# Moving one of layer 0's background modulation groups in gate/up to layer 1's projections and gate/up, in a one-core encoder trunk

## The chip, the cores and the metric

The kernel runs on one core of one Trainium2 chip. The metric is the device time of one execution in microseconds, the median of several runs. A profile of one execution, taken by the hardware profiler, stands beside it.

## The reference

Two layers of a bidirectional encoder over 1024 tokens of width 1024, in fp32. Each layer draws six vectors of length 1024 (the modulation: shift, scale and gate for the attention part and for the feed-forward part) from a condition vector `c`. A group, in this document, is one such vector of one layer: group `(l, g)` is layer `l`'s vector number `g` from 0 to 5.

```
cond = silu(c)                                   # (1024,)
for l in range(2):
    mod = cond @ w_mod[l] + b_mod[l]             # (6 * 1024,): a matrix of 1024 x 6144
    sh_a, sc_a, gt_a, sh_f, sc_f, gt_f = split(mod, 6)     # groups (l, 0) .. (l, 5)
    h = rms_norm(x, g_attn[l]) * (1 + sc_a) + sh_a
    proj = h @ w_in[l]
    y = concat of three attention groups (neighbourhood, sliding window, dense), each normalized
    x = x + gt_a * (y @ w_o[l])
    h = rms_norm(x, g_ffn[l]) * (1 + sc_f) + sh_f
    gate, up = split(h @ w_gu[l], 2)             # two times 2816 columns
    x = x + gt_f * ((silu(gate) * up) @ w_down[l])
return rms_norm(x, g_final)
```

## The kernel before

**Matmuls.** Every fp32 operand is split into a high part, rounded for the fast matmul, and a low part, the rest; a product is three matmuls (high x high, low x high, high x low). ScalarE (ACT) makes the high parts by a copy, VectorE (DVE) or GpSimd (POOL) the low parts by a subtraction. The helper that records every operation is line 49, so the profile puts all of them on L49; they are told apart by their tiles.

**Gate/up.** The product of `h` with `w_gu` is cut by a Strassen-like scheme into seven products for each of 22 blocks of columns, counted by `q` (even `q` a gate block, odd `q` the up block that belongs to it). The seven are listed in `PRODUCTS` (line 218) and run in the order h11, h21, ht2, ht1, ht3, h22, ht4, named for the operand made from `h`; their place in the list is `i`, 0 to 6. One product of one `q` is called a unit here: 12 matmuls into a PSUM tile `ps_w` (`product`, `gu_product`). ACT reads the results out of PSUM (tile `u`, or `sg`) and takes the Silu; DVE and POOL add the pieces, multiply gate by up (tiles `u` and `sg`), and the finished blocks are stored to DRAM (`gpd`) through SyncE's queue (SP). The weights of a block arrive in `wr` through the same queue; DVE makes the sums of weight blocks (`ws`), and ACT, DVE and POOL their high and low parts (`wpt`), a few units ahead (`Ahead.fill`). A product waits for its `wpt` parts, and for ACT to have read the PSUM tile that it writes into.

The first seven blocks (`EARLY = 7`) have their first two products done ahead of the loop; from `q = 7` on a block's seven units follow each other, 105 units in all.

**Modulation beside it.** Groups are worked off in the order of a list `todo`. The first two of layer 0 are computed at the start. The others run in the background, as a matrix-vector product on DVE: a load of a piece of `w_mod` (tile `wmt`), then `acc += wmt * cond[k]` on DVE, and when a group's rows are through, a sum over the 128 partitions. That sum (`mod_parts`, line 325, and `mod_flush`, line 334) is: DVE copies half of `acc` to `acch` and subtracts to get `accl`; PE multiplies both with a matrix of ones (tile `ps_mod`, two matmuls, one reduction pair); DVE multiplies by the identity and reduces along the free axis (`sums`); then the same for the other half. `mod_finish` adds the bias, and for a scale group (g = 1 or 4) one product gives `gsc`.

There are two places for this work. In a layer's projections (`mod_one`, line 1082) 24 steps of one row block each work off three groups per layer. In gate/up `mod_stream` (line 358) is a generator that is advanced one step at a time behind a unit:

```
            halves = [(k, c0) for k in range(first, KC) for c0 in range(0, 1024, width)]
            ...
            for i, (k, c0) in enumerate(halves):
                if i + 1 < len(halves):
                    load(i + 1)
                mod_add(k, acc[:, c0 : c0 + width], loads.pop(i))
                yield
            going["step"] = KC
            mod_parts(slice(0, width), shared)
            while going["step"]:
                yield
                yield
                mod_flush(psp)
            yield
```

`width` is 512, so a group has 16 halves. A group takes 22 steps: one that only loads, 16 adds, and five for the two reduction pairs. `mod_parts` issues the copies `acch` and `accl`; two steps later `mod_flush` issues the pair on PE that reads them, and in the same step `mod_parts` for the second half. The loads go into a tag with two buffers, so the load of a half waits for the add two before it.

**What sets the order.** Instructions are issued in program order, one queue per engine, and in gate/up a scheduling layer may reorder ACT's, DVE's, POOL's and PE's; SP's order is pinned to the program's in this loop (`pin([sp], True)`), so every load and store of gate/up, of `wr`, `gpd` and `wmt`, stands in one line. An engine's instructions start in the order of its queue. In the loop a unit's product comes first, then `ahead.fill()`, then `g_step()` (a piece of the block's finishing), then the modulation step (line 2060).

The loop before, line 2015 and lines 2059 to 2062: the stream runs up to, not including, group (1, 3), in whichever layer; a step follows every unit from `q = 7` on; what is left is run off behind the loop.

Of the kernel before, what the change touches and what calls it, by code (L numbers as in the profile page):

```python
# [23 lines left out]
H = 512  # L24
# [61 lines left out]
def trunk(ctx: ExitStack, tc, A, C, out):  # L86
# [9 lines left out]
    def open_pool(name, bufs=1, side="left", space=None):  # L96
        kw = dict(name=name, bufs=bufs, side=side, reuse_waits="tile")
        if space is not None:
            kw["space"] = space
            if space == PSUM:  # L100
                kw.pop("side")
        cm = tc.tile_pool(**kw)
        p = cm.__enter__()
        return cm, p
# [200 lines left out]
    def mod_add(k, acc, st):  # L305
        ck = condT[:, k : k + 1]
        if k == 0:
            dve.tensor_scalar(out=acc, in0=st, scalar1=ck, scalar2=None, op0=ALU.mult)
        else:
            dve.scalar_tensor_tensor(  # L310
                out=acc, in0=st, scalar=ck, in1=acc, op0=ALU.mult, op1=ALU.add
            )
# [12 lines left out]
    def mod_parts(c, shared):  # L325
        pl, tag, bufs, width = shared
        acc = going["acc"]
        hi = pl.tile([P, width], F32R, name="acch", tag=tag, bufs=bufs)
        lo = pl.tile([P, width], F32R, name="accl", tag=tag, bufs=bufs)
        dve.tensor_copy(hi, acc[:, c])  # L330
        dve.tensor_tensor(out=lo, in0=acc[:, c], in1=f32(hi), op=ALU.subtract)
        going["parts"] = c.start, hi, lo, shared

    def mod_flush(psp):

        if going["step"] < KC:
            return
        acc, (c0, hi, lo, shared) = going["acc"], going["parts"]
        width = shared[3]
        if c0 == 0:  # L340
            going["sums"] = cp.tile([P, 8], F32, name="sums", tag="sums")
        sums = going["sums"]
        for o in range(0, width, H):
            ps = psp.tile([P, 4, P], F32, name="ps_mod", tag="mm")
            row = ps.rearrange("p a b -> p (a b)")
            pe.matmul(row, onesr, hi[:, o : o + H], start=True, stop=False)
            pe.matmul(row, onesr, lo[:, o : o + H], start=False, stop=True)
            d = acc[:, c0 + o : c0 + o + H].rearrange("p (a b) -> p a b", a=4)
            dve.tensor_tensor(out=d, in0=ps, in1=bc(ident[:, None, :], [P, 4, P]), op=ALU.mult)
            n = (c0 + o) // P  # L350
            dve.tensor_reduce(out=sums[:, n : n + 4], in_=d, axis=AX.X, op=ALU.add)
        if c0 + width < 1024:
            mod_parts(slice(c0 + width, c0 + 2 * width), shared)
            return
        mod_finish(*todo.pop(0), sums)
        going["step"] = 0

    def mod_stream(psp, shared, until):


        pl, tag, bufs, width = shared
        acc = None
        while todo and todo[0] < until:
            l, g = todo[0]
            first = going["step"]
            if first == 0:
                going["acc"] = cp.tile([P, 1024], F32, name="acc", tag="acc")
            acc = going["acc"]
            halves = [(k, c0) for k in range(first, KC) for c0 in range(0, 1024, width)]
            loads = {}  # L370

            def load(i):
                k, c0 = halves[i]
                st = loads[i] = pl.tile([P, width], F32, name="wmt", tag=tag, bufs=bufs)
                g0 = g * 1024 + c0
                sp.dma_start(st, A["w_mod"][l, k * P : (k + 1) * P, g0 : g0 + width])

            if halves:
                load(0)
# [13 lines that stand above are left out]
# [140 lines left out]
    ps_cm, psl = open_pool("ps0", bufs=8, space=PSUM)  # L533
# [285 lines left out]
    for l in range(2):  # L819
# [353 lines left out]
        for oc in range(NE, 8):  # L1173
            w = wab
            for half in range(2):
# [3 lines left out]
                if oc == 6 and half == 0:  # L1179
                    close(ps_cm)  # L1180
                    psS_cm, psS = open_pool("psS", bufs=2, space=PSUM)
                    ps_cm, psl = open_pool("ps2", bufs=4, space=PSUM)
# [8 lines left out]
                i = 2 * (oc - NE) + half  # L1191
# [404 lines left out]
        for n in range(-AHEAD - 1, N + 3):  # L1596
# [70 lines left out]
            for end, (chunks, width) in norms.items():  # L1667
                if begins[end] <= m <= end and (m - begins[end]) % 8 == 7 and (n <= NC or m >= NC):
                    i = (m - begins[end]) // 8
# [29 lines left out]
        ps_cm, psl = open_pool("ps1", bufs=4, space=PSUM)  # L1699
# [65 lines left out]
        nt_cm, ntp = open_pool("nt", side="left")  # L1765
# [80 lines left out]
        ps_cm, psl = open_pool("ps3", bufs=8, space=PSUM)  # L1846
# [110 lines left out]
        def g_step():  # L1957
            if steps:
                steps[0].pop(0)()
                if not steps[0]:  # L1960
                    steps.pop(0)
# [6 lines left out]
        def gu_start(b):  # L1968
            g_finish(1)
            sg[b] = [x_tile(4 + 2 * (b % 2) + i, [P, S], "sg") for i in range(2)]  # L1970
# [11 lines left out]
        EARLY = 7  # L1982
# [29 lines left out]
            shifted_sub(b21, b21, shift(2 * i + 1), t2)  # L2012
            h_split("t4", i, b21, dve)

        mods_due = mod_stream(psl, (ntp, "sq", 2, H), (1, 3))
        bs = []
        rows = None
        norm = rstd_rows(ssq, ntp, psl)
# [24 lines left out]
        for q in range(NF):  # L2043
            if q % 2 == 0:
                gu_start(q // 2)
            if q < EARLY:
                up = q % 2
                e = sg[q // 2][0][:, 0:H]
                if up:
                    (pool if q > 1 else dve).tensor_tensor(  # L2050
                        out=e, in0=e, in1=quads[q]["11"], op=ALU.mult
                    )
            for i, p in enumerate(PRODUCTS[2 if q < EARLY else 0 :]):
                gu_product(q, p, ahead.get())
                if i == 1 and q < EARLY and not up:
                    act.activation(e, quads[q]["11"], AF.Silu)
                ahead.fill()
                g_step()
                if q >= EARLY:
                    next(mods_due, None)  # L2060
        for _ in mods_due:
            pass
# [30 lines left out]
        nt_cm, ntp = open_pool("nt", side="left")  # L2093
# [134 lines left out]
        for u in range(NU):  # L2228
            i, t = divmod(u, NB)
# [161 lines left out]
```

## Time and profile before

| | |
|---|---|
| median of 3 runs | 2412.68 us (2412.14 to 2415.06) |
| profiled execution | 2419.0 us, span 2417.2 us |
| mean granted TensorE clock | 0.991 |
| busy share of the span: PE, DVE, ACT, POOL | 97%, 73%, 49%, 31% |
| gate/up from the first to the last ps_w matmul, layer 0 | 586.6 to 1023 us |
| the same, layer 1 | 1763.5 to 2187 us |

In a timeline row stand the start in us, the length, the engine, the operation with output and input tiles, and in brackets the idle time ahead of it with what ended it. Matmuls are pipelined: one is shown with about 0.39 us, while the next starts 0.23 us later, so the distance between starts is what counts. A row of the waits has the engine and tile, what it waited for, the us in total, the number of times and the longest.

### The profile page before, as it was taken

What the parts mean: (1) busy time and instruction counts of PE and PEld (TensorE: products, weight loads), DVE (VectorE), ACT (ScalarE), POOL (GpSimd) and SP (SyncE); (2) the same over time, 40 slices, a digit from 0 to 9 for tenths busy, and PEclk for the clock granted to TensorE, in tenths of its full rate; (3) what the DMA queues carried; (4) which work ended last, traced back from release to release, by engine and by line L of the source; (5) the groups of instructions that cost most, each with busy time, mean ns of one, the idle gap of its engine ahead of it and who ended that gap; (6) DMA issues with size and microseconds to landing.
All of it is one profiled execution on the core that took longest, in us unless ns stands there. A gap on an engine that the chain in (4) does not pass through costs nothing.

```text
span 2417.2 us, 33362 instructions
## 1 busy us (share of the span) xinstructions
PE 2343.7 (97%) x11733; PEld 1957.8 (81%) x11733; DVE 1756.8 (73%) x2788; ACT 1194.7 (49%) x2250; POOL 744.0 (31%) x719
## 2 busy tenths in 40 slices
PE   8999999999999999999999999999999999999998
PEld 4777899888788787788787879988888888888886
DVE  5756898977967788587578579988797545447865
ACT  3421688954543333344444138897454333334443
POOL 1430345720144444300037114465004444430001
PEclk9999999999999999999999999999999999999999
DMA  8478215254245454596433861151534332329633
GB/s 264 143 235 274 71 27 133 58 178 149 92 144 179 157 182 153 158 285 191 138 110 97 282 198 32 27 161 61 196 99 160 116 101 96 121 90 298 212 129 109
DMA packets 305336, 356.95 MB, mean 148 GB/s; under 512 B 51964, under 2 KB 221788, under 8 KB 305168
## 3 DMA queue, kind: packets, MB, share of 16 engines
q1 hardware_dynamic: 283296, 342.07, 44.5%
q10 hardware_dynamic: 21504, 12.59, 2.0%
q8 instruction: 92, 1.51, 0.2%
q14 instruction: 76, 0.62, 0.1%
q0 software_dynamic: 368, 0.17, 0.0%
HBM read 269.79 MB, written 88.63 MB: 148 GB/s over the span
## 4 chain that ended last, share of the span: by engine, by line
PE 45%; DVE 5%; issue 4%; DMA 4%; ACT 3%; POOL 1%; SPq 0%; ACTq 0%; POOLq 0%; DVEq 0%
PE ps_w L49 21%; PE ps_d L49 11%; PE ps_o L49 3%; PE pv L49 2%; PE T L49 2%; PE ps_v L49 2%; PE sC L49 2%; DMA qkd<-qko 1%; DVE wpt L49 1%; ACT pr L49 1%; DMA w<-in_w_down_dram 1%; PE ps_c L49 1%; DMA cst<-const_rope_dram 1%; DMA graw<-gpd 1%; DVE xb L49 0%
## 5 line engine op out<-in xcount | busy, mean ns | idle before, releaser
L49 PE MATMUL ps_d<-wpt 128*128 128x512 f32 x1848 | 424.3, 390 | 4.0 <-ACT wpt L49 3.4
L49 PEld LDWEIGHTS ps_d<-wpt 128*128 128x128 f32 x1848 | 345.5, 188 | 78.1 <-issue 3.3
L49 POOL TENSOR_SCALAR pr<-pr,rs 128x1024 f32<-128x1024 f32 (+2 forms) x248 | 193.7, 794 | 219.3 <-DVE rs L49 190.3
L49 POOL TENSOR_TENSOR sg<-sg,u 128x512 f32<-128x512 f32 x82 | 116.5, 1421 | 353.6 <-ACT sg L49 227.8
L49 PE MATMUL pv<-pt,vs 128*128 128x256 f32 x1088 | 175.5, 296 | 17.2 <-DVE y L49 13.3
L49 DVE TENSOR_TENSOR pt<-T,pt 128x512 fp32r<-128x512 f32 x272 | 176.8, 678 | 7.4 <-ACT pt L49 7.1
L49 ACT CAST wpt<-w 128x512 fp32r<-128x512 f32 x154 | 95.9, 622 | 170.5 <-PE ps_d L49 153.1
L49 ACT CAST pt<-T 128x512 fp32r<-128x512 f32 x272 | 152.3, 585 | 40.7 <-PE T L49 38.6
L49 ACT COPY u<-ps_w 128x512 f32<-128x512 f32 x128 | 75.2, 587 | 189.9 <-PE ps_w L49 189.9
L49 POOL TENSOR_TENSOR wpt<-ws,wpt 128x512 fp32r<-128x512 f32 x80 | 110.4, 1381 | 186.2 <-ACT wpt L49 139.8
L49 DVE TENSOR_TENSOR wpt<-w,wpt 128x512 fp32r<-128x512 f32 x154 | 109.4, 710 | 79.5 <-ACT wpt L49 79.3
L49 PEld LDWEIGHTS pv<-pt,vs 128*128 128x128 f32 x1088 | 141.4, 189 | 30.0 <-DVE y L49 25.6
L49 PE MATMUL T<-identr,pr 128*128 128x128 f32 x1176 | 161.6, 273 | 0.9 <-DVE edge L49 0.4
L49 DVE SCALAR_TENSOR_TENSOR acc<-wmt,condT,acc 128x512 f32<-128x512 f32 (+1 forms) x98 | 117.2, 1204 | 47.0 <-DMA wmt<-in_w_mod_dram 46.3
L49 PEld LDWEIGHTS T<-identr,pr 128*128 128x128 f32 x1176 | 137.9, 140 | 16.1 <-issue 1.4
L49 ACT CAST wpt<-ws 128x512 fp32r<-128x512 f32 x176 | 108.1, 624 | 59.8 <-issue 28.2
L49 DVE TENSOR_TENSOR wpt<-ws,wpt 128x512 fp32r<-128x512 f32 x96 | 81.8, 861 | 62.1 <-ACT wpt L49 62.0
L49 DVE TENSOR_TENSOR wpt<-graw,wpt 128x512 fp32r<-128x512 f32 x154 | 110.3, 716 | 21.3 <-ACT wpt L49 21.1
L49 ACT CAST wpt<-graw 128x512 fp32r<-128x512 f32 x154 | 95.2, 618 | 60.0 <-DMA graw<-gpd 50.5
L49 DVE TENSOR_REDUCE rs<-sC 128x1 f32<-128x1024 f32 x88 | 107.3, 1221 | 17.8 <-PE sC L49 13.7
L49 DVE TENSOR_TENSOR ws<-wr 128x512 f32<-128x512 f32 x88 | 78.9, 899 | 54.2 <-POOL wpt L49 51.1
L49 PE MATMUL sC<-qk 128*128 128x512 f32 x384 | 108.9, 407 | 6.4 <-ACT pr L49 6.4
(300 smaller groups left out, 5945.7 us busy)
## 6 DMA issues: line engine op xcount, KB each, us to landing
wr<-in_w_gu_dram SPq DMA_DIRECT2D x92, 512.0 KB, 4.2
gpd<-sg SPq DMA_DIRECT2D x154, 256.0 KB, 4.4
graw<-gpd SPq DMA_DIRECT2D x76, 512.0 KB, 3.5
w<-in_w_down_dram SPq DMA_DIRECT2D x110, 256.0 KB, 5.1
wmt<-in_w_mod_dram SPq DMA_DIRECT2D x48, 512.0 KB, 6.1
qk<-qkd SPq DMA_DIRECT2D x44, 512.0 KB, 6.6
wst<-in_w_o_dram SPq DMA_DIRECT2D x32, 512.0 KB, 3.9
wmt<-in_w_mod_dram SPq DMA_DIRECT2D x64, 256.0 KB, 3.7
```

What stands on the lines that cost most here:

```text
L49: ins = op(*args, **kwargs)
```

## The change

```
-        mods_due = mod_stream(psl, (ntp, "sq", 2, H), (1, 3))
+        mods_due = mod_stream(psl, (ntp, "sq", 2, H), (1 + l, 2 - 2 * l))
...
                 ahead.fill()
                 g_step()
-                if q >= EARLY:
+                if q >= EARLY and i % 3 != 2:
                     next(mods_due, None)
         for _ in mods_due:
             pass
```

The bound of the stream is (1, 2) in layer 0 and (2, 0), the end of the list, in layer 1. Layer 0's projections do three groups as before, (0, 2) to (0, 4). Its gate/up did four, (0, 5) and (1, 0) to (1, 2); now it does three, up to (1, 1). Layer 1's projections did (1, 3) to (1, 5); now they do (1, 2) to (1, 4). Layer 1's gate/up, which did none, does (1, 5), the gate of the last residual. In gate/up no step follows the units i = 2 and i = 5, so five of a block's seven units have one.

The first place is DVE's queue in layer 0's gate/up, in the two reductions of the first group there, (0, 5): `acch` and `accl` are the copies that PE's pair reads, `acc<-ps_mod` is the reading of a pair's result, `ws` and `wpt` are weights, `sg` and `u` are gate/up's results. Before, from the first half's low part on:

```order
854 L49 TENSOR_TENSOR accl<-acc,acch 128x512
855 L49 TENSOR_TENSOR wpt<-ws,wpt 128x512
856 L49 TENSOR_TENSOR ws<-wr 128x512
857 L49 TENSOR_TENSOR ws<-ws,wr 128x512
858 L49 TENSOR_TENSOR wpt<-ws,wpt 128x512
859 L49 TENSOR_TENSOR ws<-wr 128x512
860 L49 TENSOR_TENSOR ws<-wr,ws 128x512
861 L49 TENSOR_TENSOR u<-u,ps_w 128x512
862 L49 TENSOR_TENSOR acc<-ps_mod,identr 128x512
863 L49 COPY acch<-acc 128x512
864 L49 TENSOR_REDUCE sums<-acc 128x4
865 L49 TENSOR_TENSOR accl<-acc,acch 128x512
```

And now, from the last rows ahead of the second half's copy to the reading of its pair:

```order
870 L49 TENSOR_TENSOR ws<-wr,ws 128x512
871 L49 TENSOR_TENSOR sg<-sg,ps_w 128x512
872 L49 TENSOR_TENSOR wpt<-wr,wpt 128x512
873 L49 COPY acch<-acc 128x512
874 L49 TENSOR_TENSOR acc<-ps_mod,identr 128x512
875 L49 TENSOR_TENSOR accl<-acc,acch 128x512
876 L49 TENSOR_REDUCE sums<-acc 128x4
877 L49 TENSOR_TENSOR wpt<-wr,wpt 128x512
878 L49 TENSOR_TENSOR u<-u,ps_w 128x512
879 L49 TENSOR_TENSOR acc<-ps_mod,identr 128x512
```

The second half's copy stood behind the first pair's reading; it now stands ahead of it, and the low part ahead of the reduction. Between the first half's `accl` (row 862 now) and the second half's `acch` stand ten rows where there were eight, over three units where there were two.

The second place is SP's queue in layer 1's gate/up, from `q = 7` on. Before:

```order
403 L49 DMA gpd<-sg 128x512 x7
404 L49 DMA wr<-in_w_gu_dram 128x4x256 x2
405 L49 DMA gpd<-sg 128x512
406 L49 DMA wr<-in_w_gu_dram 128x4x256 x2
407 L49 DMA gpd<-sg 128x512 x6
408 L49 DMA wr<-in_w_gu_dram 128x4x256 x2
```

Now:

```order
401 L49 DMA gpd<-sg 128x512 x7
402 L49 DMA wr<-in_w_gu_dram 128x4x256 x2
403 L49 DMA wmt<-in_w_mod_dram 128x512 x3
404 L49 DMA gpd<-sg 128x512
405 L49 DMA wmt<-in_w_mod_dram 128x512
406 L49 DMA wr<-in_w_gu_dram 128x4x256 x2
407 L49 DMA gpd<-sg 128x512 x2
408 L49 DMA wmt<-in_w_mod_dram 128x512
409 L49 DMA gpd<-sg 128x512
410 L49 DMA wmt<-in_w_mod_dram 128x512 x2
411 L49 DMA gpd<-sg 128x512 x3
412 L49 DMA wmt<-in_w_mod_dram 128x512 x2
```

The loads of the moved group stand between the stores of gate/up's results and the loads of its weights, which the queue had to itself in this layer.

More of the change, by code (lines that the diff above doesn't have):

```diff
@@ L2013, in t4_part @@
             h_split("t4", i, b21, dve)
-        mods_due = mod_stream(psl, (ntp, "sq", 2, H), (1, 3))
+        mods_due = mod_stream(psl, (ntp, "sq", 2, H), (1 + l, 2 - 2 * l))
         bs = []
@@ L2058, in trunk @@
                 g_step()
-                if q >= EARLY:
+                if q >= EARLY and i % 3 != 2:
                     next(mods_due, None)
```

## The prediction

> **What bounds the kernel now.** I read the page first, then the chain that ended last, then the busy time by stretches, then the PE timeline of both layers.
>
> ```profile
> PE 2343.7 (97%) x11733; PEld 1957.8 (81%) x11733; DVE 1756.8 (73%) x2788; ACT 1194.7 (49%) x2250; POOL 744.0 (31%) x719
> PE 45%; DVE 5%; issue 4%; DMA 4%; ACT 3%; POOL 1%; SPq 0%; ACTq 0%; POOLq 0%; DVEq 0%
> ```
>
> PE is busy for 97% of the span, so a change that leaves PE's work alone can only gain where PE stands still or runs at less than its pace. The change touches gate/up from the eighth unit column (q = 7) on, in both layers. The windows compare these stretches: 724 to 1016 is layer 0 with four modulation groups beside it, 1900 to 2177 is layer 1 with none. The columns are us, PE, PEld, DVE, ACT and POOL busy, granted clock, DMA share, GB/s. The third row is the same view for the instructions on the tile wmt (the modulation adds) alone.
>
> ```profile
> 724.00:1016.00 292.00, 286.70 (x1251) 235.32 (x1251) 218.19 (x268) 105.48 (x188) 123.71 (x85) 0.99 0.49 160
> 1900.00:2177.00 277.00, 277.00 (x1224) 229.37 (x1223) 134.62 (x168) 106.42 (x187) 114.41 (x85) 1.00 0.32 104
> 724.00:1016.00 292.00, 65.48 (x64) 0.99 0.49 160
> ```
>
> DVE works 218.2 of 292 us in layer 0 and 134.6 of 277 us in layer 1; PE has no idle time at all in layer 1's stretch. The PE timeline gives the exact length: first matmul of q = 7, and the ht3 product of the last q, which are 102 products apart in both layers.
>
> ```profile
> 724.05 0.62 PE L49 MATMUL ps_w<-h11h,wpt 128*128 128x512 f32 x2
> ...
> 1013.86 0.61 PE L49 MATMUL ps_w<-ht3h,wpt 128*128 128x512 f32 x2
> ...
> 1900.35 0.61 PE L49 MATMUL ps_w<-h11h,wpt 128*128 128x512 f32 x2
> ...
> 2177.79 0.62 PE L49 MATMUL ps_w<-ht3h,wpt 128*128 128x512 f32 x2
> ```
>
> Layer 1 takes 277.44 us, 2.72 us a unit; layer 0 takes 289.81 us for the same products. The four groups thus cost PE 12.37 us, and this is all that the change can play with. Where they lie:
>
> ```profile
> 778.46 0.39 PE L49 MATMUL ps_mod<-acch,onesr 128*128 128x512 f32 x1
> 778.69 0.39 PE L49 MATMUL ps_mod<-accl,onesr 128*128 128x512 f32 x1
> 778.92 0.63 PE L49 MATMUL ps_w<-ht4h,wpt 128*128 128x512 f32 x2
> ...
> 784.17 0.39 PE L49 MATMUL ps_w<-h11l,wpt 128*128 128x512 f32 x1
> 785.73 0.51 PE L49 MATMUL ps_mod<-acch,onesr 128*128 128x512 f32 x1 [1.18 <-DVE acch L49]
> 787.70 0.54 PE L49 MATMUL ps_mod<-accl,onesr 128*128 128x512 f32 x1 [1.46 <-DVE accl L49]
> 788.04 1.05 PE L49 MATMUL ps_w<-h21h,wpt 128*128 128x512 f32 x2
> ...
> 792.38 0.62 PE L49 MATMUL ps_w<-ht2h,wpt 128*128 128x512 f32 x2
> ...
> 910.63 0.39 PE L49 MATMUL ps_w<-ht2l,wpt 128*128 128x512 f32 x1
> 911.51 0.50 PE L49 MATMUL ps_mod<-acch,onesr 128*128 128x512 f32 x1 [0.49 <-DVE acch L49]
> 912.71 0.50 PE L49 MATMUL ps_mod<-accl,onesr 128*128 128x512 f32 x1 [0.69 <-DVE accl L49]
> 913.04 0.63 PE L49 MATMUL ps_w<-ht1h,wpt 128*128 128x512 f32 x2
> ...
> 967.84 0.40 PE L49 MATMUL ps_mod<-accl,onesr 128*128 128x512 f32 x1
> 969.71 0.73 PE L49 MATMUL ps_w<-ht2h,wpt 128*128 128x512 f32 x2 [1.47 <-ACT u L49]
> ```
>
> Without a wait matmuls start 0.23 us apart, and a reduction pair takes 778.46 to 778.92, 0.46 us; eight pairs are 3.68 us. The pair at 785.73 comes late: 1.33 us before it (784.17 to 785.73 less 0.23), 1.74 inside it, 0.11 behind it, and the next product takes 788.04 to 792.38, 4.34 us in place of 2.72, another 1.62. That is 4.80 us. The pair at 911.51 loses 0.65 + 0.97 + 0.10 = 1.72. At 969.71 a product waits 1.87 less 0.23 = 1.64 for ACT. Together 8.16 us; 12.37 - 3.68 - 8.16 = 0.53 stays unassigned.
>
> The 1.62 us come from the granted clock, in the columns of the windows above:
>
> ```profile
> 784.00:788.00 4.00, 1.36 (x5) 0.62 (x4) 4.00 (x6) 1.10 (x2) 2.53 (x2) 1.00 0.08 27
> 788.00:792.00 4.00, 4.00 (x12) 3.09 (x11) 2.79 (x6) 0.00 (x0) 0.00 (x0) 0.57 0.79 271
> ```
>
> PE worked 1.36 of 4.00 us, and the four us behind were granted 0.57 of the clock.
>
> Why DVE is late: it is in order, and an add that waits for its load holds the copies acch and accl that PE then waits for. ACT's late reading is the same lag at second hand; a Silu there waited for DVE and four other operations stood behind it, one of them the reading that PE needed.
>
> ```profile
> DVE acc L49 <- DMA wmt<-in_w_mod_dram: 42.2, 27, 5.2
> ...
> 967.54 0.64 ACT L49 ACTIVATE sg<-sg 128x512 f32<-128x512 f32 x1 [6.91 <-DVE sg L49]
> ...
> 969.07 0.59 ACT L49 COPY u<-ps_w 128x512 f32<-128x512 f32 x1
> ```
>
> DVE in layer 0's stretch is therefore taken for 218.2 + 42.2 = 260.4 of 292 us, 89%.
>
> **The change part by part.** *The group that leaves layer 0.* On DVE a group is 16 adds and the two reductions. The adds of four are 65.5 us, the reductions of four are these rows:
>
> ```profile
> L49 DVE TENSOR_TENSOR accl<-acc,acch 128x512 fp32r<-128x512 f32 x8 | 7.8, 974 | 0.0
> L49 DVE TENSOR_REDUCE sums<-acc 128x4 f32<-128x512 f32 x8 | 5.4, 680 | 0.1
> L49 DVE TENSOR_TENSOR acc<-ps_mod,identr 128x512 f32<-128x512 f32 x8 | 5.4, 680 | 0.0
> L49 DVE CAST acch<-acc 128x512 fp32r<-128x512 f32 x8 | 5.0, 625 | 0.0
> ```
>
> So (65.5 + 7.8 + 5.4 + 5.4 + 5.0) / 4 = 22.3 us a group, and a quarter of the waits, 10.5 us. Layer 0 goes from 260 of 292 us to about 228 of 284 (80%), layer 1 from 135 of 277 to 134.6 + 22.3 + 10.5 = 167 of 280 (60%). On PE the two pairs go from one layer to the other: -0.92 and +0.92, net nothing, whatever the cover.
>
> *The step in five of seven units.* A group is 22 steps, of which the last five hold both reductions; from the copies to the pair that reads them are two steps. Before, two steps were always two units, 5.4 us. Now they are three units (8.2 us) or two, by where the left-out units i = 2 and i = 5 fall: 3 and 2 in layer 0's first group, 2 and 3 in the second, 3 and 3 in the third, 3 and 2 in layer 1. Three groups need 66 steps of 75, so they end at unit 92 of 105 rather than at 88, still ahead of the down projection; layer 1's group ends by its unit 30 (30 x 2.72 = 82 us after 1900), and its result, the gate of the last residual, is read behind 2186. So lateness costs nothing there.
>
> *The waits.* The lag that PE met at 785.73 and 911.51 was 3.07 and 1.62 us (waits before and inside the pair). Two things work against it: a unit more (2.72 us) in five of the eight pairs, and DVE at 80% and 60% in place of 89%. In the pairs that keep two units I count on the second alone: over 5.4 us nine hundredths of DVE are 0.5 us, but the backlog that stands when the copies come is built over a whole group, 16 adds that now come every 3.8 us in place of 2.72. Per term: the 4.80 is between 0 (the first group's second pair still has two units) and 4.80, and I take 4.80, since the first pair now has three units and hands on no lag; the 1.72 likewise goes (three units in the third group). The 1.64 behind ACT I leave: it hangs on a Silu behind one DVE sum, not on the two steps; one in four groups has it. For the moved group in layer 1 I bound such a wait by 0 (layer 1's row without groups) and 1.64, and take 0.9, near the middle, for it is a whole group with its loads but on an emptier DVE.
>
> *SP.* The moved group brings 16 loads of 256 KB to layer 1's queue, between the loads of the next weights (wr) and the stores of gate/up; each add's buffer holds up what is queued behind its load. In layer 0 this queue carried 64 of them:
>
> ```profile
> SPq L49 <- DVE acc L49: 43.4, 39, 3.2
> wmt<-in_w_mod_dram SPq DMA_DIRECT2D x64, 256.0 KB, 3.7
> ```
>
> 43.4 us of such holding in 39 cases, and yet no PE wait above names a load of weights. Layer 1 gets a quarter of that, and I cost it at nothing; the cover is that weights are loaded a whole column ahead. Without it each case could pass on up to its longest, 3.2 us.
>
> *Layer 1's projections.* They still do 24 steps, of the groups two, three and four in place of three, four and five: same shapes, same queue, only the small gsc product changes place. I cost that at nothing on PE either way.
>
> *Sum.* 2419.0 - 4.80 - 1.72 + 0.90 = 2413.4 for the profiled execution (span 2417.2 and 1.8 around it). The profiled execution lies 6.3 us above the median of 2412.68, so the forecast is 2412.68 - 5.62 = **2407.1 us**. Its own range is from all 8.16 and the 0.53 gone (2404.0) to half of 6.52 gone (2409.4).
>
> **Rivals.** 0.2% is 4.8 us, about what a measurement of this kernel can tell from no change.
>
> *The wait changes its place.* PE is tied to DVE's lag, and the lag to loads that DVE waits for; each group keeps its mean price of 8.16 / 4 = 2.04 us, in layer 1 too. For it: the longest wait for a load is 5.2 us, longer than the 3.8 us between steps. Against it: two of four groups had next to no wait. Time: 2412.7, give or take 2.
>
> *Half speed by chance.* The drop of 1.62 us hung on where the gap fell in time. The three timed runs lie 2.9 us apart, more than one such drop, so the runs without a profile may have had none; and the gap at 911.51 (1.72 us) and the one at 969.71 brought no drop. Then only 5.62 - 1.62 = 4.0 are gained: 2408.7. [...]
>
> *Slower: the start of a group makes the lag, not its density.* The moved group then meets in layer 1 what the first group met in layer 0, 4.80, and the wait behind ACT, 1.64, while layer 0 keeps what it had: +6.4, 2419.1. It decides if DVE's backlog, when the copies come, is still over two units, 5.4 us, in a layer where DVE is 60% taken. Against it: layer 1's DVE has 277 - 135 = 142 us free.
>
> **How the numbers follow.** Forecast 0.70; of its range 2404.0 to 2409.4 about two thirds lie below 2407.9, so 0.48 faster and 0.22 the same. Place changed 0.14, all but 0.01 of it the same. Half speed 0.08, the same. Slower rival 0.08. That gives faster 0.48, same 0.43, slower 0.09. The range 2404.0 to 2412.5 leaves out the slower rival, half of the second and a little below.
>
> **What would show it.** Right: in layer 0 no wait of ps_mod for acch or accl over 0.3 us and a clock of 1.00 around 788; the distance from the first product of q = 7 to the last ht3 shrinks from 289.8 to about 283.3 us less the 0.92 that moved, 282.4, and grows in layer 1 from 277.4 to about 279.3; waits of DVE for wmt fall below 42.2 us in both layers together. Wrong: a PE wait on ACT of over 2 us in either layer, a wait of ps_mod in layer 1, a wait for wpt behind SP's queue, or a changed time outside gate/up.

## The result and the profile after

The changed kernel takes 2406.19 us (median of 22 runs, 2402.56 to 2412.89) beside 2412.09 us for the kernel before (22 runs): a ratio of 0.9977, 95% interval 0.9970 to 0.9984. A second measurement, described below, gave 2409.10 beside 2412.79: 0.9984, 0.9975 to 0.9994. The forecast was 2407.1. Both measurements lie around the prediction's bound of 0.2%: a gain of 4 to 6 us. Of all runs told of here one, of the kernel with later pairs, took 3328.93 us at a granted clock of 0.65, and it is left out of that kernel's time.

The busy shares of the span (part 1 of the page) have hardly moved: PE is busy for 97% as before, with the same 11733 matmuls, and DVE for 73%.

Where the time went is read from the two stretches that the prediction compared, from the first product of q = 7 to the last ht3. In the PE timeline of the changed kernel they are these:

```profile
716.11 0.62 PE L49 MATMUL ps_w<-h11h,wpt 128*128 128x512 f32 x2
...
998.45 0.62 PE L49 MATMUL ps_w<-ht3h,wpt 128*128 128x512 f32 x2
...
1885.48 0.62 PE L49 MATMUL ps_w<-h11h,wpt 128*128 128x512 f32 x2
...
2165.74 0.62 PE L49 MATMUL ps_w<-ht3h,wpt 128*128 128x512 f32 x2
```

Layer 0 takes 282.34 us (before 289.81), layer 1 280.26 (before 277.44): -7.47 and +2.82, together -4.65. The start of q = 7 lies 8 us earlier than in the profile of before, but in code that the change does not touch, and over all the kernels below it lies between 716 and 724. Ahead of it the mean granted clock was 0.98 in the profile of before and 0.99 here, and a hundredth of the clock over 720 us is about 7 us (an estimate). So spans of single profiles are not compared, only the stretches.

What PE waits for in layer 0, and then in layer 1 (us in total, times, longest):

```profile
PE ps_w L49 <- ACT sg L49: 0.9, 2, 0.7
PE ps_w L49 <- ACT u L49: 0.9, 1, 0.9
...
PE ps_w L49 <- ACT sg L49: 0.5, 1, 0.5
PE ps_w L49 <- ACT u L49: 0.4, 1, 0.4
```

No wait of `ps_mod` for `acch` or `accl` is left in either. The 0.9 on `u` in layer 0 stands at 1002.18, behind the stretch. The clock was 1.00 over both stretches. The window at the us of the old gap shows it (seventh number from the left, behind the five engines), with PE at work for 3.80 of 4.00 us:

```profile
784.00:788.00 4.00, 3.80 (x17) 2.92 (x16) 3.90 (x5) 2.38 (x5) 1.34 (x1) 1.00 0.00 0
```

And DVE's waits for the loads of `w_mod`, in layer 0 and in layer 1, did not fall. They rose, from 42.2 to 69.1 us, for 64 loads in both kernels:

```profile
DVE acc L49 <- DMA wmt<-in_w_mod_dram: 49.4, 25, 5.3
...
DVE acc L49 <- DMA wmt<-in_w_mod_dram: 19.7, 9, 5.2
```

So the waits of PE went as forecast, but not by a DVE that waits less. What made them go is the question of the experiments.

### The profile page after: what moved, and what is told of

Same layout as the page of the kernel before. It is cut to its first block, busy times and chain, and to the rows that moved or that the text cites. A ratio compares the mean times of both kernels' runs of the same rounds, so it can differ in the third digit from the quotient of the medians.

```text
span 2405.6 us, 33338 instructions
## 1 busy us (share of the span) xinstructions
PE 2337.1 (97%) x11733; PEld 1953.7 (81%) x11733; DVE 1754.7 (73%) x2788; ACT 1191.6 (50%) x2250; POOL 747.6 (31%) x719
## 3 DMA queue, kind: packets, MB, share of 16 engines
q8 instruction: 92, 1.51, 0.3%
## 4 chain that ended last, share of the span: by engine, by line
PE 67%; DVE 11%; DMA 8%; ACT 5%; issue 5%; POOL 2%; SPq 1%; ACTq 0%; POOLq 0%; DVEq 0%
PE ps_w L49 28%; PE ps_d L49 12%; PE ps_o L49 7%; PE pv L49 5%; PE T L49 4%; PE ps_v L49 3%; PE sC L49 3%; DMA qkd<-qko 3%; ACT pr L49 2%; DMA wmt<-in_w_mod_dram 2%; PE ps_c L49 1%; DVE wpt L49 1%; PE ps_ab L49 1%; DVE acc L49 1%; DVE ws L49 1%
## 5 line engine op out<-in xcount | busy, mean ns | idle before, releaser
L49 PE MATMUL pv<-pt,vs 128*128 128x256 f32 x1088 | 175.6, 296 | 17.4 <-DVE y L49 13.5
```

What stands on the lines that cost most here:

```text
L49: ins = op(*args, **kwargs)
```

## The experiments

Two theories at first. **Lag**: DVE falls behind over a group, since its adds come at every unit and wait for loads; fewer steps and more units between the copies and the pair cure it. **Place**: only where a group happens to end among the other work matters. The tables' "stretches" are the two distances above, from one profile each.

| kernel | layer 0 | layer 1 | sum, against before | time against before, 95% |
|---|---|---|---|---|
| before | 289.81 | 277.44 | | |
| the change | 282.34 | 280.26 | -4.65 | 0.9977 (0.9970 to 0.9984) |
| the change again | 283.04 | 279.40 | -4.81 | 0.9984 (0.9975 to 0.9994) |
| bound moved only | 288.96 | 281.79 | +3.50 | 1.0014 (1.0002 to 1.0026) |
| steps thinned only | 281.55 | 277.44 | -8.26 | 1.0081 (1.0059 to 1.0102) |
| before, pairs two steps later | 295.74 | 277.44 | +5.93 | 1.0016 (1.0007 to 1.0024) |
| moved, pairs one step later | 285.54 | 279.94 | -1.77 | 1.0009 (1.0000 to 1.0018) |
| the change, pairs one step nearer | 284.50 | 279.64 | -3.11 | 0.9995 (0.9984 to 1.0006) |
| steps left out behind 0 and 4 | 281.49 | 279.80 | -5.96 | 0.9973 (0.9962 to 0.9983) |
| moved, begun 8 units later | 284.38 | 279.41 | -3.46 | 0.9986 (0.9972 to 0.9999) |
| the change, GpSimd issues the loads | 311.39 | 288.90 | +33.04 | 1.0146 (1.0131 to 1.0161) |

**Each half alone.** The move without the thinning:

```
-        mods_due = mod_stream(psl, (ntp, "sq", 2, H), (1, 3))
+        mods_due = mod_stream(psl, (ntp, "sq", 2, H), (1 + l, 2 - 2 * l))
```

> The bound of the stream is changed as in the change, a step still follows every unit. Theory (PE loses its time where a reduction pair is issued two units after its copies while DVE is behind, and it takes fewer groups and wider steps together to mend it): layer 0 keeps the late pairs of its first and third group (4.80 and 1.72 us) and loses only the wait that its fourth group brought (1.64), and layer 1's group, which stands at the same units as layer 0's first, pays 4.80 there: 0 to 4 us slower than before, about 2414; ps_mod waits for acch and accl in both layers. Rival A (fewer groups on layer 0's DVE are what counts): 5 to 6 us faster, about 2406.5, without waits of ps_mod. Rival B (only the wider steps count): no change, 2412, with layer 0's waits as before and none in layer 1.

Measured 2417.22 (11 runs) beside 2413.11: slower. PE's waits in layer 0, and then in layer 1:

```profile
PE ps_mod L49 <- DVE accl L49: 2.1, 2, 1.4
PE ps_mod L49 <- DVE acch L49: 2.1, 2, 1.2
...
PE ps_mod L49 <- DVE acch L49: 1.6, 1, 1.6
PE ps_mod L49 <- DVE accl L49: 1.2, 1, 1.2
```

Layer 0 keeps both late pairs of before, since its first three groups are what they were, and the moved group meets one of its own in layer 1, as late as in layer 0. Over the whole stretch DVE is busy there for only 154.8 of 283 us. So the mean density of a stretch, with which the prediction reckoned, cannot be the cause. A lag that is built up within one group is not refuted yet: in the 60 us of the group DVE is as full as in layer 0, busy for 44.8 us and waiting 14.6 us for loads, beside 44.3 and 15.0.

And the thinning without the move:

```
-                if q >= EARLY:
+                if q >= EARLY and i % 3 != 2:
                     next(mods_due, None)
```

> Four groups stay in layer 0, a step follows five of seven units. 88 steps do not fit into 75, so 13 are run off behind the loop with no product beside them: half of the last group's adds and both its reductions. Theory: the waits of the first three groups go as in the change (6 to 7 us less), but the 13 bare steps hold PE, which reads ps_mod before the down projection: 8 adds of 1.1 us, their loads and two reductions of about 3 us, 10 to 15 us; in sum 3 to 8 us slower than before, about 2417. Rival B (the wider steps alone are the gain, the tail is covered): 5 to 6 us faster, 2406.5. Rival A (fewer groups count): no gain in the first three groups, and the tail on top, 2422 or more.

Measured 2433.25 (5 runs), 20 us slower, more than expected. Inside the stretch it does as well as the change, 281.55 us and no late pair. But four groups need 88 steps and get 75; the other 13 run off behind the loop, where nothing hides them. The PE timeline there:

```profile
1017.54 0.79 PE L49 MATMUL ps_mod<-acch,onesr 128*128 128x512 f32 x1 [7.18 <-DVE acch L49]
1020.75 0.79 PE L49 MATMUL ps_mod<-accl,onesr 128*128 128x512 f32 x1 [2.42 <-DVE accl L49]
1022.76 0.76 PE L49 MATMUL ps_mod<-acch,onesr 128*128 128x512 f32 x1 [1.21 <-DVE acch L49]
1024.92 1.65 PE L49 MATMUL ps_d<-wpt 128*128 128x512 f32 x3 [1.40 <-ACT wpt L49]
```

These are 12.2 us of waits, and the clock that was granted from 1013.7 to 1030.8 us was 0.50. From the start of the last product to the first `ps_d` matmul pass 17.4 us, before 2.7. The same profile has another 9.15 us in layer 1's projections, where PE waits for a DVE held by a load of `w_mod`; before and the change have no such wait there, and whether it belongs to this edit stays open. Neither half gains: the thinning needs the move so that its groups end inside the loop.

**The distance alone.** The kernel before with four steps rather than two ahead of each `mod_flush`:

```
             while going["step"]:
                 yield
                 yield
+                yield
+                yield
                 mod_flush(psp)
```

> The kernel before, but with four steps rather than two from the copies acch and accl to the reduction pair; a group takes 26 steps, four of them 104 of 105. DVE has the same work. Rival C (only the distance from copies to pair counts): the waits of ps_mod, 3.07 and 1.62 us, and the half clock behind the first go and nothing comes in their place: 5 to 6.5 us faster, 2406. Theory (DVE's lag is the cause, the pair only one of the places where PE meets it): no wait of ps_mod, but products wait for ACT, which waits for DVE's sums, as at 969 us in the kernel before, by 3 to 6 us in sum: between 3 us faster and 2 us slower, about 2411.

Measured 2417.06 (11 runs): the late pairs are gone, and the loss is larger, for another reader of DVE's results is now the late one. Rival C falls. The theory has the mechanism, but PE loses more than its 3 to 6 us. The ACT timeline and PE's next product:

```profile
991.34 0.63 ACT L49 ACTIVATE sg<-u 128x512 f32<-128x512 f32 x1 [11.36 <-DVE u L49]
...
992.50 1.22 PE L49 MATMUL ps_w<-ht3h,wpt 128*128 128x512 f32 x2 [7.78 <-ACT sg L49]
```

A Silu waits 11.36 us for a sum on DVE, whose queue ahead of it holds adds, copies and sums of blocks with one pause of 1.08 us; behind the Silu stands the copy out of PSUM that PE needs.

**Distance and thinning crossed.** With three groups in layer 0, the move with one more `yield` ahead of `mod_flush`, and the change with one fewer:

> The bound as in the change, a step behind every unit, and three steps (three units, 8.2 us) rather than two between the copies acch and accl and the pair that reads them. Theory A (distance): the pair only has to come later than DVE's lag; the pairs' waits go though DVE's adds come as densely as before. Layer 0's stretch from 289.8 (before) to about 282, a time of 2406 to 2409. Rival B (density): adds that come at every unit leave DVE behind all through the group, and with the pair out of the way the lag shows in ACT's readings, as in the kernel with later pairs and four groups (12 us of waits behind ACT there); three quarters of that, some 4 to 9 us, leave layer 0's stretch at 284 to 289 and the time at 2410 to 2416.

> The change with one step rather than two between the copies and the pair: one or two units (2.7 or 5.4 us) in place of two or three. Theory A (distance): the pairs find the copies missing again; ps_mod waits of 1 to 4 us at most of the eight pairs, a time of 2412 to 2420. Rival B (density): thinner adds keep DVE up to date, a copy and its low part need 625 + 974 ns, and 2.7 us hold both; next to no ps_mod wait, 2405 to 2408.

The first measured 2413.76 (11 runs), with layer 0 at 285.54: no late pair, but two waits of PE behind ACT in layer 0, 2.1 and 2.0 us. Both numbers are rival B's (284 to 289 us, 2410 to 2416); its reason, density, is tested by the shift below.

The second measured 2411.68 (11 runs). Its pairs come a step sooner and none is late, against theory A; its gain is nevertheless mostly gone, in three waits behind ACT in layer 0, 3.1 us together. So the added distance isn't needed for the pairs where these groups end, and theory A falls there; but rival B's time, 2405 to 2408, was wrong as well.

**The place alone.** A group with a step at every unit takes 22 units, and gate/up's own work repeats every 14 (a gate block and its up block). The groups of before began at places 0, 8, 2 and 10 of those 14; late were the first and the third. The last experiment leaves density and distance as in the move alone and only begins later:

```
         acc = None
+        for _ in range(8):
+            yield
         while todo and todo[0] < until:
```

> The bound as in the change, a step behind every unit as before, but the stream lets the first 8 units of each layer's stretch pass. A group takes 22 units and the weights' and results' work on the other engines repeats every 14 (a gate block and its up block), so the groups began at units 0, 8, 2 and 10 of that pattern in the kernel before, and the pairs came late in the first and the third. Now they begin at 8, 2 and 10 in layer 0 and at 8 in layer 1. Theory P (place in the pattern): what begins at 8 meets no late pair, in layer 1 neither; the second group in layer 0 meets the third's of before (1.7 to 3.7 us), the third group the wait of 1.6 us behind ACT; layer 0's stretch 284 to 286.5, layer 1's 278.4 to 279.5, and a time 3 to 7 us under that of the move alone (2417.2, 1.0014 of before), so 0.9985 to 1.0002 of before. Theory D (density: adds at every unit make DVE late, wherever the group stands): late pairs in layer 1 and in layer 0's first group as with the move alone, 289 and 281.8 us, and its time, 1.0005 to 1.0025 of before.

Measured 2410.08 (12 runs) beside 2413.97: 0.9986, where the move without the shift had 1.0014. Layer 1 has no late pair (279.41 us). Layer 0 has the one that was forecast, in the group that begins at 2, and the wait behind ACT in the group that begins at 10 (the waits of PE in layer 0):

```profile
PE ps_w L49 <- ACT u L49: 1.5, 1, 1.5
PE ps_mod L49 <- DVE accl L49: 0.7, 1, 0.7
PE ps_mod L49 <- DVE acch L49: 0.5, 1, 0.5
```

284.38 and 279.41 us lie in theory P's 284 to 286.5 and 278.4 to 279.5, and outside theory D's. Place decides whether a pair is late, with DVE as densely loaded as before: in the 60 us of layer 0's first group it is busy for 46.1 us and waits 12.5 us for loads, where the move alone had 44.3 and 15.0. That refutes the lag that is built up over a group.

What is at place 0 can now be read. DVE in the kernel before, from the low part of the first half to that of the second, and below it GpSimd in the same us:

```profile
774.57 1.77 DVE L49 TENSOR_TENSOR accl<-acc,acch 128x512 fp32r<-128x512 f32 x1
776.26 0.68 DVE L49 TENSOR_TENSOR wpt<-ws,wpt 128x512 fp32r<-128x512 f32 x1
777.03 1.61 DVE L49 TENSOR_TENSOR ws<-wr 128x512 f32<-128x512 f32 x1
778.68 1.68 DVE L49 TENSOR_TENSOR ws<-ws,wr 128x512 f32<-128x512 f32 x1
780.28 1.78 DVE L49 TENSOR_TENSOR wpt<-ws,wpt 128x512 fp32r<-128x512 f32 x1
782.16 0.69 DVE L49 TENSOR_TENSOR ws<-wr 128x512 f32<-128x512 f32 x1
...
784.57 1.11 DVE L49 CAST acch<-acc 128x512 fp32r<-128x512 f32 x1
...
776.65 1.44 POOL L49 TENSOR_TENSOR u<-u 128x512 f32<-128x512 f32 x1 [0.86 <-ACT u L49]
778.17 1.64 POOL L49 TENSOR_TENSOR sg<-sg,u 128x512 f32<-128x512 f32 x1
779.77 1.74 POOL L49 TENSOR_TENSOR wpt<-wr,wpt 128x512 fp32r<-128x512 f32 x1
```

From the end of `accl` (776.34) to the second `acch` (784.57) DVE needs 8.2 us, without a wait for any load. Three rows run beside GpSimd and take 1.61, 1.68 and 1.78 us where the same shapes take 0.68 to 0.69; the excess is 5.07 - 2.07 = 3.0 us, as much as the whole lag of 3.07 us that PE met. The third group, at place 2, has two such rows right ahead of its copy, 3.18 us in place of 1.36, beside a lag of 1.62 us:

```profile
908.01 1.41 DVE L49 TENSOR_TENSOR wpt<-wr,wpt 128x512 fp32r<-128x512 f32 x1
909.34 1.77 DVE L49 TENSOR_TENSOR sg<-sg 128x512 f32<-128x512 f32 x1
911.04 0.42 DVE L49 CAST acch<-acc 128x512 fp32r<-128x512 f32 x1
...
908.83 1.74 POOL L49 TENSOR_TENSOR wpt<-wr,wpt 128x512 fp32r<-128x512 f32 x1
```

With the move alone layer 1 has the same rows in the same order: 1.61, 1.67 and 1.78 us from 1947.09 on, and the second copy at 1954.61.

In the kernel begun 8 units later the same stretch of the first group is

```profile
795.95 0.68 DVE L49 TENSOR_TENSOR accl<-acc,acch 128x512 fp32r<-128x512 f32 x1
796.55 0.68 DVE L49 TENSOR_TENSOR ws<-ws,wr 128x512 f32<-128x512 f32 x1
797.16 0.68 DVE L49 TENSOR_TENSOR wpt<-ws,wpt 128x512 fp32r<-128x512 f32 x1
...
800.76 0.42 DVE L49 CAST acch<-acc 128x512 fp32r<-128x512 f32 x1
...
793.13 1.75 POOL L49 TENSOR_TENSOR wpt<-ws,wpt 128x512 fp32r<-128x512 f32 x1
802.03 1.51 POOL L49 TENSOR_TENSOR wpt<-wr,wpt 128x512 fp32r<-128x512 f32 x1 [7.15 <-ACT wpt L49]
```

GpSimd rests from 794.88 to 802.03, every DVE row takes 0.68 us, and the second copy comes 4.1 us after the first half's low part.

A rival is left that the shift doesn't settle: the group at place 0 is also the first of its stretch. But the doubled rows belong to the loop and come back in every round of 14 units. In layer 1 of the kernel before, which has no group, all DVE sums of over 1.3 us but two stand in the units of places 5 to 7, and each round, 38.08 us, repeats them:

```profile
1915.34 1.37 DVE L49 TENSOR_TENSOR wpt<-ws,wpt 128x512 fp32r<-128x512 f32 x1 [3.29 <-ACT wpt L49]
1916.82 1.60 DVE L49 TENSOR_TENSOR ws<-wr 128x512 f32<-128x512 f32 x1
1918.34 1.77 DVE L49 TENSOR_TENSOR ws<-wr,ws 128x512 f32<-128x512 f32 x1
...
1954.90 1.60 DVE L49 TENSOR_TENSOR ws<-wr 128x512 f32<-128x512 f32 x1
```

In the kernel before the second halves' copies are issued behind the units of places 5, 13, 7 and 1; late are the first and the third. In the change they are issued behind places 13, 1 and 4 in layer 0 and 13 in layer 1. So three of its four groups end where the groups in time ended before. The third group of layer 0 does not. Its second half meets doubled rows too, and a copy of 1.51 us:

```profile
959.43 1.62 DVE L49 TENSOR_TENSOR ws<-wr 128x512 f32<-128x512 f32 x1
961.08 1.67 DVE L49 TENSOR_TENSOR ws<-ws,wr 128x512 f32<-128x512 f32 x1
962.67 1.51 DVE L49 CAST acch<-acc 128x512 fp32r<-128x512 f32 x1
...
966.41 1.18 DVE L49 TENSOR_TENSOR accl<-acc,acch 128x512 fp32r<-128x512 f32 x1
```

Its low part is ready at 967.59, and its pair comes at 969.72, three units behind the copies. A pair two units behind them, 2.72 us sooner, would have been some 0.6 us late (an estimate from these rows). There the added unit seems to count.

That the doubled rows are the cause is read from these rows and the sum that fits; no run moved GpSimd's work alone. What stays open is what thinner steps do by themselves: they change the places too (a group then takes some 31 units in place of 22). Nearest comes the next kernel, which leaves out other units: the second copies of its third group are issued behind place 5, the doubled rows are there (1.62, 1.66, 1.60 and 1.77 us), and the low part is ready at 971.65 for a pair at 973.44, again three units behind. No kernel has thin steps with a pair two units behind copies at place 5 or 7.

**Another choice of units.** The change with the steps left out behind i = 0 and 4:

```
-                if q >= EARLY and i % 3 != 2:
+                if q >= EARLY and i not in (0, 4):
```

> The change, but the two units of a block that no step follows are i = 0 and i = 4 in place of i = 2 and i = 5, so that no add stands on DVE right ahead of the sum of the second product, which ACT's Silu waits for. Theory (what is left in the change are waits for ACT behind late sums on DVE, 0.3 to 1.0 us each, five in the two layers): most of them go, 1 to 2.5 us faster than the change, about 2404.5, with layer 0's stretch near 281 us and layer 1's near 279. Rival (the place of the steps does not matter, only their number): as the change, 2406, with the same stretch lengths of 282.3 and 280.3 us.

> One more profile of the kernel that leaves out the steps behind i = 0 and 4, to see how far a stretch differs from one execution to the next: 281.7 in layer 0 and 279.8 in layer 1 within 0.5 us if the waits are a matter of the program's order, 1 us and more apart if they are a matter of when loads arrive.

Measured 2406.19 (10 runs), 0.9973: not to be told from the change, and no better by anything that the intervals separate. The second profile has 281.84 and 280.28 us, within 0.5 of the first; the change's two profiles differ by 0.70 and 0.86. A stretch is therefore good to about 1 us, which also limits what the table's smaller differences can carry. The kernel with moved groups and later pairs shows the limit of stretches as well: 1.77 us shorter than before, and yet measured at 1.0009. What is left of waits behind ACT has its places as well: in every kernel of the table a product in the two stretches that waits for ACT by 0.2 us or more follows a unit of place 1 or 10.

**The moved group's price in layer 1.** Two kernels were to leave it out, with layer 1's last gate set to zero:

```
+        if l:
+            dve.memset(mods[1][:, 40:48], 0.0)
```

> The change without the moved group's work in layer 1: the stream stops there at once, and the gate of the last residual is set to zero, so the output lacks layer 1's feed-forward part. Its time against the change's is what the moved group costs in layer 1 without a profile. If the 2.82 us by which layer 1's stretch grew in the profile are all: 2403.4. If loads beside the projections or behind the stretch cost as well: below 2402. If the group is hidden: 2406.

Here the stream's bound, `(2, -9)`, still lies above `(1, 5)`, so the group ran: this was the change and one small memset, and measured 2410.03 (11 runs), 0.9988 (0.9974 to 1.0001), with stretches of 282.74 and 279.43. With the bound `(1, 5)`, and the change on the same chip:

> The changed kernel once more, beside the next kernel on one chip, since the kernel meant to leave out layer 1's group (its bound let the group run after all, so that it was the change and one small memset) came out at 0.9988 of before, where the change had 0.9977. If its time is that of the first measurement: 2404 to 2408 and a ratio of 0.996 to 0.999; layer 0's stretch 282.3 and layer 1's 280.3, each within 0.6.

> The change without the moved group in layer 1's gate/up: the stream stops ahead of it, and the gate of the last residual is set to zero, so the output lacks layer 1's feed-forward part. Against the change on the same chip it gives what the moved group costs. If the 2.82 us by which layer 1's stretch grew in the profile are all, layer 1's stretch is 277.4 and the time 2.8 us under the change's; if the group's loads beside the stretch cost as well, over 4 us under it; if its cost is hidden elsewhere, no difference.

The change measured 2409.10 (12 runs), the kernel without the group 2408.39 (11 runs), 0.9986 (0.9974 to 0.9997) of before. Layer 1's stretch is 278.40 without the group and 279.40 with it, so on this chip the moved group costs about 1 us, not 2.8. But a stretch is good to about 1 us, and the kernel without the group lost 0.96 us in two places where the one with it lost none. Row by row, what 279.40 has over the 277.44 of before is 0.92 us for the two pairs and 0.93 for one wait behind ACT. Its price thus lies between 1 and 2.8 us. In time the two kernels can't be told apart.

**The loads' queue.**

```
-                sp.dma_start(st, A["w_mod"][l, k * P : (k + 1) * P, g0 : g0 + width])
+                pool.dma_start(st, A["w_mod"][l, k * P : (k + 1) * P, g0 : g0 + width])
```

> The change with the stream's wmt loads issued through GpSimd's queue rather than SyncE's; the scheduler then also puts the adds in other places of DVE's queue. If DVE's waits for wmt (69.1 us in the two stretches) come from loads that stand in line behind the weights' loads and stores on SyncE's queue, they fall below 35 us, the waits of PE behind ACT go, and layer 0 and 1 come to 280.5 and 278.5: a time 3 us under the change's. If they are the transfer itself (3.9 us from issue to landing, two buffers), they stay, and GpSimd held at an issue delays weights' low parts: the change's time or up to 10 us above it.

Measured 2447.57 (4 runs), 1.0146: far worse than the 10 us of the second alternative, and the two stretches, 33 us longer than before, hold nearly all of it. In layer 0 DVE's waits for the loads fall, from 49.4 to 31.3 us, but GpSimd now waits at the issue for a free buffer, and what stands behind it is late at PE (waits of GpSimd and PE in layer 0):

```profile
POOL wmt L49 <- DVE acc L49: 47.4, 29, 4.0
...
PE ps_w L49 <- ACT sg L49: 20.8, 4, 6.3
```

DVE waits less for loads and PE waits more: in this kernel the sum of DVE's waits for `wmt` says nothing about PE.

## Why the prediction was right, and where it was not

- *PE's 12.37 us in layer 0 are all there is to gain.* Nothing speaks against it: -4.65 to -4.81 us in the stretches is 0.19 to 0.20% of the time, beside a measured 0.16 to 0.23%.
- *The 4.80 and the 1.72 us go.* Right in size: no late pair, clock 1.00, 282.34 us for a forecast 282.4 (283.04 in the second profile).
- *Why they go: the step that failed.* The prediction held that DVE's lag is built up over a group by adds that wait for loads, and that a unit more between copies and pair and a DVE at 80 and 60% cure it. Between the copies of the late pair there is no wait for a load. The shifted kernel has neither thinner steps nor more distance, its DVE is as full over the group, and the pairs of the groups that no longer begin at place 0 are in time. With the move alone DVE in layer 1 is near the 60% that was counted on, and PE waits 1.6 + 1.2 us for the pair's parts. In its place: in the groups that begin at places 0 and 2 of the 14-unit pattern the second half's copy stands behind DVE rows that run beside GpSimd at double length (1.41 to 1.78 us in place of 0.68 to 0.69), and the change moved the ends of three of its four groups away from there. That the place decides is shown; that it does so through GpSimd is read from the rows. One part of the prediction's cure may have held: the change with nearer pairs has no added unit and no late pair, but its groups end at other places, and in the change's third group the rows leave room for the added unit to count.
- *Waits for wmt fall below 42.2 us.* Wrong: 69.1. That a DVE with fewer steps arrives sooner at an add and waits there would explain it; no run tests that. These waits grew while the pairs' waits went, so their sum does not tell whether a pair comes late.
- *1.64 us behind ACT stay in layer 0.* Right in sum, by other waits. Behind the unit where the 1.64 stood, 0.18 is left (0.61 in the second profile), and new waits of 0.36 and 0.89 us (0.65 and 0.89) stand behind two units of place 10. The rows at 979.27 in layer 0, with 0.73 us, and at 1955.16 in layer 1, with 0.50, name ACT's `sg`, a copy out of PSUM behind a Silu that waited 4.30 and 4.08 us for one DVE sum, as in the reasoning.
- *0.9 us in layer 1, with 0.92 for the pairs: 279.3.* Measured 280.26 and 279.40: the second profile agrees, the first is a us over. That the middle of two bounds, 0 and 1.64, came so close is luck: no row of the kernel before shows such a wait in layer 1.
- *SP's loads and layer 1's projections at nothing.* Nothing in the waits speaks against it: PE waits for no `wpt` behind SP's queue in either stretch. From the last ht3 of layer 0 to q = 7 of layer 1 pass 886.49 us before and 887.03 and 887.20 in the change.
- *The rivals.* Wait changes its place (2412.7): no. Half speed by chance (2408.7): it can't be told from the forecast by time, and the clock rows at the end of this document speak for its chance: with the move alone the late pair of layer 1 brought no drop. That the drop hung on where its gap fell in time was the author's assumption; no run shows what sets it off. The gap ahead of the one drop in these stretches of the kernel before was in two pieces, the longest idle time 1.46 us, and PE worked for 1.36 of the 4.00 us. The sum also reckons with no drop behind the waits that it leaves, 1.64 and 0.9 us. Behind the 1.64 in the kernel before the clock was 1.00 (970 to 974 us), and in the change, with waits of up to 0.89 us left, it was 1.00 over both stretches. The slower one, that the start of a group makes the lag, was nearer to the truth than its 0.08: with the move alone it came true in layer 1, +4.35 us, for another reason than it gave. The change escaped it, as far as the rows show, because the thinning also shifts where groups end.

The number came out right because the forecast rested on which waits exist. That they would go was in part luck: by the places, neither the emptier DVE nor, in three of the four groups, the added unit was needed, and the prediction did not look at the places to which the thinning moves the groups' ends.

## What to carry to other kernels

Before blaming an engine's load for a late operand, read the rows between the last thing it delivered in time and the late one: here they held no wait for a load, but three rows at double length (1.61, 1.68 and 1.78 us in place of 0.68 to 0.69) beside GpSimd's. Background work whose period doesn't divide the loop's meets different neighbours in every round; shift it by a few units, or thin it, and measure the places, rather than its mean density over a stretch. Parts of such a change are not additive: the move alone (1.0014) and the thinning alone (1.0081) both lost time, and the 13 steps that didn't end inside the loop cost PE 12.2 us of waits.

## What the runs showed of the hardware

Most DVE sums of 128 x 512 shown above beside GpSimd took 1.37 to 1.78 us, without it 0.68 to 0.69, and GpSimd's own rows there took 1.44 to 1.74 us where single ones in layer 1 of the kernel before took 1.28 to 1.30. DVE sums that read one of their inputs from PSUM (`sg<-sg,ps_w`, `u<-u,ps_w`, `acc<-ps_mod,identr`) took 0.68 to 0.69 us beside GpSimd too, in layer 0 of that kernel. That the price, 3 us at one place, was as large as the lag of the costliest pair was not expected.

The clock went to half, 0.50, after a shorter gap than the profile of before showed. With the move alone, windows of 2 us around the second late pair read (the number ahead of the last two is the granted clock):

```profile
908.00:910.00 2.00, 0.63 (x2) 0.19 (x1) 2.00 (x4) 0.00 (x0) 0.01 (x1) 1.00 0.91 256
910.00:912.00 2.00, 1.84 (x6) 1.53 (x7) 2.00 (x5) 0.07 (x1) 0.00 (x0) 0.75 0.04 11
912.00:914.00 2.00, 2.00 (x6) 1.51 (x6) 1.97 (x4) 1.55 (x3) 0.37 (x1) 0.50 0.00 0
```

PE had lost 2.07 us there, in two pieces, and then 1.62 us to the clock; the same pair in the kernel before lost 1.72 us and nothing to the clock. So 2.07 us, with matmuls between, were enough there. And a longer gap brought no drop: at the late pair of layer 1 in the same profile PE lost 3.29 us, and the clock stayed at 1.00:

```profile
1954.00:1958.00 4.00, 1.26 (x4) 0.67 (x4) 4.00 (x7) 1.10 (x2) 2.63 (x2) 1.00 0.59 210
1958.00:1962.00 4.00, 4.00 (x19) 3.29 (x18) 3.97 (x7) 0.62 (x1) 0.00 (x0) 1.00 0.61 196
```

In the kernel before, PE worked for 1.36 of the 4.00 us from 784 on, and 0.57 of the clock was granted behind; here it worked for 1.26 and lost nothing to the clock. In these profiles neither the length of a gap nor the share of work in it tells of the drop by itself.
